# SSD scan of a two-block layer: earlier loads of decays and gates, stores moved to ScalarE's queue, input transposes in one-bank tiles

## Chip, cores, metric

The kernel runs on one core of one Trainium2 chip. The metric is device time in microseconds (us), the median of three runs; lower is better. The engines are named as in the profile: PE (TensorE matmul), PEld (its weight loads), DVE (VectorE), ACT (ScalarE), POOL (GpSimd), SP (SyncE, which here only issues transfers).

## What is computed

A sequence of 1024 tokens of width 1024 in fp32 passes through two blocks. The first block has a recurrent and attention layer and then an SSD (state space) layer; the second has a feed-forward part, a mixing layer and another feed-forward part. The change is in the SSD layer, whose scan works in 8 chunks of 128 tokens, for 4 groups of 8 heads:

```python
proj = x @ w_in                                   # z, xbc, dt
xs, bm, cm = split(silu(causal_conv(xbc)))        # inputs, B and C states
cs = cumsum(dt * a_neg) within a chunk
decay = exp(cs[l] - cs[s]) where s <= l
y_diag = ((C B^T) * decay) @ (xs * dt)            # inside a chunk
states = B^T @ (xs * dt * exp(cs[last] - cs))
y_off  = (C @ prev) * exp(cs); prev = prev * exp(cs[last]) + states
y = (y_diag + y_off + d_skip * xs) * silu(z)      # z: the gates
y = y * rsqrt(mean(y * y) per group) * norm_w
out = y @ w_out
```

## The kernel before

Every fp32 operand of a large product is split into a high and a low part, so a product is three matmuls (high with high, high with low, low with high). A scheduler puts the instructions of each engine into one fixed order when the kernel is built; `turn` and `issue_after` fix the order on PE. Each engine, and the queue of transfers on SP, works through its own list in order.

The SSD layer goes through 4 groups. A group has ten projection units, i = 0 to 9: two for B and C (`states`), four for the inputs (`inputs`), four for the gates (`gates`). A unit fills a two-bank PSUM tile `a` from a pool of two (`K.A`); ACT reads it out (L353 and L354 of the convolution, or L900 for a gate, which is then stored to DRAM at L901). `tokens` (L907) turns an input unit's result to tokens by rows: eight transposes (L914) into one more tile of `K.A`, two copies by ACT (L916).

While the units of group g run, the chunks of group g - 1 are worked off, one at the end of each unit (`chunk`, L992). Chunk n is made of:
- `within(n)`, called one chunk ahead: the decay row is loaded, spread over 128 partitions (L933, 512 KB), into a tile `s` of a pool of two; POOL subtracts (L934), DVE clips (L935), ACT takes the exponential (L936); PE makes C B^T and a transpose into a one-bank tile `pb` (L938, L939) of a pool of four (`K.B`); POOL scales the inputs (L942 to L944).
- `heads(n)`: 16 small matmuls (L952), added to y by DVE (L953).
- `between(n)`: the part from earlier chunks (L961, L962), the new state (L966, L968, L969), then the load of the chunk's gates (L972, 256 KB) into the buffer `xw`.
- `norm(n)`: y times gates on DVE (L976), square and sum on ACT (L978), the reciprocal root on DVE (L264 to L293), scaling on ACT (L980). `chunk(n)` calls `norm(n - 1)`.
- `flip(n)`: four transposes (L987) into `pb`, a copy on ACT (L988) and a store from SP (L989). It runs in the middle of the unit, two chunks later.

The last group's chunks have no units beside them. There, `early(i)` of `SsdOut` (L1062) is the company: 60 matmuls (L695) that multiply the rows of groups 0 to 2 that are ready with the output weights; their operands are streamed by `stream_rows` (load L708, split by ACT L140 and DVE L141), the sum is added by DVE (L1075) and stored (L1076). `prepare` (L1050) fills the weights: L1041 loads, L1043 (ACT) and L1044 (DVE) split. In the loop the order is `early(i)` with `flip(22 + i)` in its middle, then `chunk(24 + i)`. `rest` (L1078) then does the remaining rows and the layer norm.

Of the kernel before, what the change touches and what calls it, by code (L numbers as in the profile page):

```python
# [14 lines left out]
AF = mybir.ActivationFunctionType  # L15
ALU = mybir.AluOpType
AX = mybir.AxisListType

P = 128
# [148 lines left out]
def turn(K, trace):  # L168

    with K.tc.issue_after(anchor(K)):  # L170
        trace()
# [621 lines left out]
def ssd_layer(K, I, get, yd, out):  # L793

    nc = K.nc
# [28 lines left out]
    cs_d = K.DR([32, T])  # L824
# [24 lines left out]
    sz_d = [K.DR([T, 512]) for _ in range(4)]  # L849
    rf = [t.rearrange("p a b -> p (a b)") for t in (K.R2(), K.R2(), K.P2())]  # L850
    hv = lambda t: t.rearrange("p (h d) -> p h d", h=8)
    groups, held = {}, {}

    def column(c0, mid=None):
        a = K.A()
# [3 lines left out]
    def units(g):  # L859
        S = groups[g] = Ctx()  # L860
        S.fs = []

        def states(j, mid):
            c0, cj = ((4096 + g * P, 16 + g), (4608 + g * P, 20 + g))[j]
            if j == 0:
                S.bc = K.Q2()
            a = first if (g, j) == (0, 0) else column(c0, mid)
            conv4(K, S.bc[:, j, :], a, "s_conv_w", cj, 24, "s_conv_b", copy=True)
            nc.scalar.activation(S.bc[:, j, :], S.bc[:, j, :], AF.Silu)

        def inputs(m, mid):
            a = column(2048 + g * 512 + m * P, mid)
            f = K.L()
            conv4(K, f, a, "s_conv_w", 4 * g + m, 24, "s_conv_b", copy=True)
            nc.scalar.activation(f, f, AF.Silu)
            S.fs.append(f)

        def gates(hf, h, mid):
            if h == 0:
                c0 = g * 512 + hf * 256  # L880
                S.w = [wload(K, w_in[:, 4 * k:4 * k + 4, c0:c0 + 256], 4, 256) for k in range(2)]
            a = K.A()

            def quarters(qs):
                for q in qs:
                    o = a[:, q * 256:q * 256 + 256]
                    tk = slice((4 * h + q) * P, (4 * h + q + 1) * P)
                    for k in range(NK):
                        wh, wl = (S.w[k // 4][m][:, k % 4, :] for m in range(2))
                        xh, xl = get("h", k)[:, tk], get("l", k)[:, tk]  # L890
                        nc.tensor.matmul(o, xh, wh, start=k == 0, stop=False)  # L891
                        nc.tensor.matmul(o, xh, wl, start=False, stop=False)  # L892
                        nc.tensor.matmul(o, xl, wh, start=False, stop=k == NK - 1)  # L893

            quarters((0, 1))
            if mid is not None:
                turn(K, mid)
            turn(K, lambda: quarters((2, 3)))
            z = K.L()
            nc.scalar.activation(z, a, AF.Silu)  # L900
            nc.sync.dma_start(sz_d[g][4 * h * P:4 * h * P + 512, hf * 256:hf * 256 + 256].rearrange("(q p) c -> p q c", p=P),  # L901
                              z.rearrange("p (q c) -> p q c", q=4))

        return ([lambda mid, j=j: states(j, mid) for j in range(2)] + [lambda mid, m=m: inputs(m, mid) for m in range(4)]
                + [lambda mid, hf=hf, h=h: gates(hf, h, mid) for hf in range(2) for h in range(2)])

    def tokens(g, m):  # L907
        S = groups[g]
        if m == 0:
            mk = K.Q2 if g % 2 else K.P2  # L910
            S.xs = [mk().rearrange("p a (b c) -> p (a b) c", b=2) for _ in range(2)]
        b = K.A()
        for q in range(8):
            nc.tensor.transpose(b[:, q * P:(q + 1) * P], S.fs[m][:, q * P:(q + 1) * P], K.ident)  # L914
        for h in range(2):
            nc.scalar.activation(S.xs[h][:, :, m * P:(m + 1) * P],  # L916
                                 b[:, 512 * h:512 * h + 512].rearrange("p (q t) -> p q t", q=4), AF.Copy)

    def cols(g, c):
        k0 = (c % 2) * 128 + (c // 2) * 32 + 8 * g  # L920
        return lambda t, n: t[:, k0:k0 + 8].unsqueeze(2).to_broadcast([P, 8, n])

    def within(n):
        g, c = divmod(n, 8)
# [3 lines left out]
        X = groups[g].xs[c // 4][:, c % 4, :]  # L928
        r = rf[n % 3]
        xdt, xw, y, cbm, bt = r[:, 0:512], r[:, 512:1024], r[:, 1024:1536], r[:, 1536:1664], r[:, 1664:1792]  # L930
        m = K.S()
        mv = m.rearrange("p (h l) -> p h l", h=8)
        nc.sync.dma_start(mv, cs_d[8 * g:8 * g + 8, c * P:(c + 1) * P].partition_broadcast(P))  # L933
        nc.gpsimd.tensor_tensor(mv, mv, per_head(csT, P), ALU.subtract)  # L934
        nc.vector.tensor_scalar(m, m, 0.0, None, ALU.min)  # L935
        nc.scalar.activation(m, m, AF.Exp)  # L936
# [18 lines left out]
    def between(n):  # L955
# [8 lines left out]
        if c < 7:  # L964
# [4 lines left out]
                nc.vector.tensor_tensor(prev, prev, st, ALU.add)  # L969
            else:  # L970
                nc.vector.tensor_copy(prev, st)
        nc.sync.dma_start(xw, sz_d[g][c * P:(c + 1) * P, :])  # L972

    def norm(n):
        _, _, xdt, sz, y, _ = held[n]
        nc.vector.tensor_tensor(y, y, sz, ALU.mult)  # L976
        t = K.small(2, "yss", bufs=3)
        nc.scalar.activation(xdt, y, AF.Square, accum_out=t[:, 0:1])  # L978
        rsqrt_col(K, t[:, 1:2], t[:, 0:1], 1, 1.0 / 512, 1e-6)
        nc.scalar.activation(y, y, AF.Copy, scale=t[:, 1:2])  # L980

    def flip(n):
# [3 lines left out]
        for q in range(4):  # L986
            nc.tensor.transpose(yt[:, q * P:(q + 1) * P], y[:, q * P:(q + 1) * P], K.ident)  # L987
        nc.scalar.activation(xw, yt, AF.Copy)  # L988
        nc.sync.dma_start(yd[4 * g:4 * g + 4, :, c * P:(c + 1) * P].rearrange("m p t -> p m t"),  # L989
                          xw.rearrange("p (m t) -> p m t", m=4))  # L990

    def chunk(n):  # L992
        heads(n)
        between(n)
        if n % 8 < 7:
            within(n + 1)
        if n % 8:
            norm(n - 1)

    for g in range(4):
        for i, unit in enumerate(units(g)):
            n = 8 * g - 8 + i
            mid = (lambda n=n: flip(n - 2)) if g and i > 1 else None
            with K.tc.issue_after(anchor(K)) if g + i else nullcontext():
                unit(mid)
            if g == 0 and i == 4:
                turn(K, steps)
            if g and i < 8:  # L1010
                turn(K, lambda: chunk(n))
            if 3 <= i < 7:
                turn(K, lambda: tokens(g, i - 3))
            if g and i == 8:
                norm(n - 1)
            if i == 8:
                turn(K, lambda: within(8 * g))
    out.prepare()
    for i in range(NT):
        turn(K, lambda: out.early(i, (lambda: flip(22 + i)) if i > 1 else None))  # L1020
        turn(K, lambda: chunk(24 + i))
    norm(31)
    return flip


class SsdOut:
# [20 lines left out]
    def half(self, i):  # L1047
        return self.yh[:, 512 * (i % 2):512 * (i % 2) + 512]

    def prepare(self):  # L1050
        K = self.K
        self.an = [anchor(K)] * 2
        xw = [K.X() for _ in range(4)]
        for k in (8, 9):
            self.fill(k)
        for k in range(8):
            self.fill(k, xw[k // 4][:, k % 4, :], xw[2 + k // 4][:, k % 4, :])
        for k in (10, 11):
# [19 lines left out]
    def rest(self, flip):  # L1078
# [14 lines left out]
        for i in range(NT):  # L1093
# [4 lines left out]
            with deferred(K, an[i]):  # L1098
                yv = dict(zip((10, 11), stream_rows(K, self.yd, 10, i, self.half(i), n=2)))
                yv.update(zip(range(12, 16), stream_rows(K, self.yd, 12, i)))  # L1100
                nc.sync.dma_start(z, self.zd[i * P:(i + 1) * P, :])
            out_tile(K, a, [w[k] for k in order], lambda k: yv[order[k]], 6, 3, (lambda: flip(30 + i)) if i < 2 else None)
            an.append(anchor(K))
            nc.vector.tensor_tensor(z, z, a, ALU.add)
            layernorm(K, z, g, b, i < 6)
# [856 lines left out]
```

## Time and profile before

| | us |
|---|---|
| median of 3 runs | 3326.03 (3321.61 to 3326.29) |
| the profiled execution, device time | 3326.46 |
| its span in the trace | 3324.6 |
| PE busy | 3087.2 (93% of the span) |
| DVE busy | 2226.4 (67%) |
| ACT busy | 1626.6 (49%) |
| POOL busy | 780.1 (23%) |
| projection units of the SSD layer | 540 to 1126 |
| its last group's chunks, beside `early` | 1126 to 1312 |

Times in the rows count from the start of the span. A busy PE is not a PE at its peak, since matmuls overlap. A wait is idle time of an engine, put down to the work that released it. The granted clock is TensorE's, 1.00 being 2.4 GHz; its other level is 1.2 GHz.

### The profile page before, as it was taken

The page shows a single profiled execution, that of the slowest core. Times are in us where ns is not written, and L with a number is a line of the kernel's source. Part 1 is how long each engine was busy: PE and PEld are TensorE (multiplying, and loading weights), DVE is VectorE, ACT ScalarE, POOL GpSimd, SP SyncE. Part 2 cuts the span into 40 slices and gives each one's busy share as a digit, 9 for nine tenths or more (in the row PEclk, how much of TensorE's full clock was granted, in tenths as well). Part 3 has the DMA queues.
Part 4 walks back from the last instruction along what each step waited for, and adds up shares of the span by engine and source line. Part 5 has one row for each costly group of instructions (what it writes and reads, how often), then busy time and mean ns, then how long its engine had stood idle before and what let it go on. Part 6 is the DMA issues. An engine that isn't in the chain of part 4 may idle for free. (4 is left out here: it accounts for less than half of the span.)

```text
span 3324.6 us, 42105 instructions
## 1 busy us (share of the span) xinstructions
PE 3087.2 (93%) x15560; PEld 2575.9 (77%) x15560; DVE 2226.4 (67%) x3605; ACT 1626.6 (49%) x2947; POOL 780.1 (23%) x487
## 2 busy tenths in 40 slices
PE   8999899999999888789999999899898799999998
PEld 6878777878887766677778777688787588888776
DVE  6537777375848445887775689735676955555997
ACT  5526634354645422555555444642465755554442
POOL 0000011122323121532223435100000433232543
PEclk9999999999999899989999999999999899999999
DMA  3157343234435545323332620445553422224322
GB/s 128 57 194 231 104 145 89 75 86 110 102 102 100 162 136 160 101 74 127 120 122 83 234 81 3 159 141 201 144 158 118 171 76 83 89 76 139 121 83 114
DMA packets 344957, 398.96 MB, mean 120 GB/s; under 512 B 20656, under 2 KB 270640, under 8 KB 344752
## 3 DMA queue, kind: packets, MB, share of 16 engines
q1 hardware_dynamic: 344752, 396.28, 38.3%
q8 instruction: 123, 2.02, 0.2%
q14 instruction: 82, 0.67, 0.1%
HBM read 279.29 MB, written 116.92 MB: 119 GB/s over the span
## 5 line engine op out<-in xcount | busy, mean ns | idle before, releaser
L141 DVE TENSOR_TENSOR wlo<-wst,whi 128x1024 fp32r<-128x1024 f32 (+1 forms) x190 | 232.3, 1226 | 349.5 <-ACT whi L140 339.0
L185 PE MATMUL pa<-x,whi 128*128 128x512 f32 x1568 | 429.4, 395 | 14.6 <-ACT l L354 10.2
L185 PEld LDWEIGHTS pa<-x,whi 128*128 128x128 f32 x1568 | 292.1, 189 | 78.4 <-ACT l L354 11.4
L140 ACT ACTIVATE whi<-wst 128x1024 fp32r<-128x1024 f32 (+1 forms) x190 | 180.0, 949 | 345.8 <-PE pa L185 85.6
L147 ACT ACTIVATE wst<-wst,pk 128x128 f32<-128x128 f32 (+1 forms) x816 | 251.7, 392 | 187.8 <-DMA wst<-in_ffn_w_in_dram 115.5
L185 PE MATMUL pa<-x,wlo 128*128 128x512 f32 x784 | 244.1, 392 | 0.8 <-DVE wlo L141 0.7
L1268 PE MATMUL pb<-x,whi 128*128 128x512 f32 (+1 forms) x736 | 224.3, 381 | 0.3 <-DVE r L141 0.3
L1268 PE MATMUL pa<-x,whi 128*128 128x512 f32 (+1 forms) x736 | 220.2, 382 | 0.6 <-ACT p L1271 0.2
L1347 PE MATMUL pa<-wlo,whi 128*128 128x512 f32 x768 | 188.4, 403 | 15.6 <-DVE wlo L141 12.8
L1347 PE MATMUL pb<-wlo,whi 128*128 128x512 f32 x744 | 182.5, 403 | 13.4 <-DVE wlo L141 13.4
L1231 POOL TENSOR_TENSOR s<-wst 128x512 f32<-128x512 f32 x44 | 57.7, 1311 | 564.5 <-ACT wst L147 526.8
L1347 PEld LDWEIGHTS pa<-wlo,whi 128*128 128x128 f32 x768 | 148.7, 195 | 52.5 <-DVE wlo L141 17.7
L1347 PEld LDWEIGHTS pb<-wlo,whi 128*128 128x128 f32 x744 | 144.0, 195 | 48.0 <-DVE wlo L141 17.7
L934 POOL TENSOR_TENSOR s<-s,p 128x1024 f32<-128x1024 f32 x32 | 61.9, 1936 | 488.5 <-DMA s<-d 401.8
L185 PEld LDWEIGHTS pa<-x,wlo 128*128 128x128 f32 x784 | 147.4, 188 | 34.3 <-DVE wlo L141 2.4
L891 PE MATMUL pa<-whi,x 128*128 128x256 f32 x512 | 149.5, 292 | 9.0 <-ACT l L900 7.6
L1268 PEld LDWEIGHTS pa<-x,whi 128*128 128x128 f32 x736 | 135.4, 188 | 28.3 <-ACT p L1271 1.1
L1268 PEld LDWEIGHTS pb<-x,whi 128*128 128x128 f32 x736 | 136.2, 188 | 27.0 <-DVE r L141 0.5
L140 ACT ACTIVATE whi<-s 128x1024 fp32r<-128x1024 f32 x88 | 93.0, 1057 | 115.1 <-POOL s L1232 67.0
L893 PE MATMUL pa<-whi,x 128*128 128x256 f32 x512 | 146.2, 286 | 0.0
L892 PE MATMUL pa<-wlo,x 128*128 128x256 f32 x512 | 146.1, 285 | 0.0
L1268 PE MATMUL pa<-x,wlo 128*128 128x512 f32 (+1 forms) x368 | 140.0, 381 | 1.5 <-DVE wlo L141 1.5
(577 smaller groups left out, 7966.4 us busy)
## 6 DMA issues: line engine op xcount, KB each, us to landing
wst<-in_ffn_w_in_dram SPq DMA_DIRECT2D x88, 512.0 KB, 3.8
d<-l SPq DMA_DIRECT2D x83, 512.0 KB, 3.3
d<-p SPq DMA_DIRECT2D x82, 512.0 KB, 3.5
x<-d SPq DMA_DIRECT2D x128, 256.0 KB, 5.4
p<-d SPq DMA_DIRECT2D x46, 512.0 KB, 4.6
wst<-in_s_w_in_dram SPq DMA_DIRECT2D x40, 512.0 KB, 4.1
s<-d SPq DMA_DIRECT2D x32, 512.0 KB, 9.5
l<-d SPq DMA_DIRECT2D x24, 512.0 KB, 5.6
```

Source lines behind the costliest of these rows:

```text
L140: K.nc.scalar.activation(hi, src, AF.Copy)
L141: (eng or K.nc.vector).tensor_tensor(lo, src, hi.bitcast(F32), ALU.subtract)
L147: K.nc.scalar.activation(st[:, k, :], st[:, k, :], AF.Copy, scale=col(K, gain, k0 + k))
L185: K.nc.tensor.matmul(ps[:, h:h + 512], w, x[:, h:h + 512], start=k == 0 and m == 0, stop=k == n - 1 and m == 2)
L891: nc.tensor.matmul(o, xh, wh, start=k == 0, stop=False)
L892: nc.tensor.matmul(o, xh, wl, start=False, stop=False)
L893: nc.tensor.matmul(o, xl, wh, start=False, stop=k == NK - 1)
L934: nc.gpsimd.tensor_tensor(mv, mv, per_head(csT, P), ALU.subtract)
L1231: G(s1, a21, a22, ALU.add)
L1268: nc.tensor.matmul(p, l[:, k, :], r[:, k, :], start=k + m == 0, stop=k == 3 and m == 2)
L1347: nc.tensor.matmul(bank[j], th[:, a + o:a + o + P], tw[:, b:b + 512], start=c + m == 0, stop=c == n - 1 and m == 2)
```

## The change

- The decay rows are loaded by a function of their own (`decays`), called two chunks ahead: for chunks 0 and 1 before the units, for n + 2 in `chunk(n)` right after `heads(n)`.
- The gates of a chunk are loaded by `gate`, in two transfers of 128 KB into spare columns of the three working buffers: for chunk n + 1 inside `norm(n)`, right after the multiplication by the gates of n, which is now two half-width multiplications.
- `chunk(n)` calls `norm(n)` and no longer `norm(n - 1)`.
- The stores of the gates (L901) and of the outputs (L989) are issued from ACT's queue.
- `tokens` uses two one-bank tiles of `K.B`, four transposes and one copy each, and no tile of `K.A`; it runs in the middle of the next unit, behind `flip`, and no longer after the chunk.
- The weights 8 and 9 of `SsdOut` are loaded and split in unit 8 of the last group (`ahead`).
- In the last group, `chunk(24 + i)` goes ahead of `early(i)`, which has `flip(23 + i)` in its middle; `rest` has one flip left.

```diff
--- before.py
+++ after.py
@@ -849,7 +849,7 @@
     sz_d = [K.DR([T, 512]) for _ in range(4)]
     rf = [t.rearrange("p a b -> p (a b)") for t in (K.R2(), K.R2(), K.P2())]
     hv = lambda t: t.rearrange("p (h d) -> p h d", h=8)
-    groups, held = {}, {}
+    groups, held, rows = {}, {}, {}
 
     def column(c0, mid=None):
         a = K.A()
@@ -898,7 +898,7 @@
             turn(K, lambda: quarters((2, 3)))
             z = K.L()
             nc.scalar.activation(z, a, AF.Silu)
-            nc.sync.dma_start(sz_d[g][4 * h * P:4 * h * P + 512, hf * 256:hf * 256 + 256].rearrange("(q p) c -> p q c", p=P),
+            nc.scalar.dma_start(sz_d[g][4 * h * P:4 * h * P + 512, hf * 256:hf * 256 + 256].rearrange("(q p) c -> p q c", p=P),
                               z.rearrange("p (q c) -> p q c", q=4))
 
         return ([lambda mid, j=j: states(j, mid) for j in range(2)] + [lambda mid, m=m: inputs(m, mid) for m in range(4)]
@@ -909,16 +909,20 @@
         if m == 0:
             mk = K.Q2 if g % 2 else K.P2
             S.xs = [mk().rearrange("p a (b c) -> p (a b) c", b=2) for _ in range(2)]
-        b = K.A()
-        for q in range(8):
-            nc.tensor.transpose(b[:, q * P:(q + 1) * P], S.fs[m][:, q * P:(q + 1) * P], K.ident)
         for h in range(2):
-            nc.scalar.activation(S.xs[h][:, :, m * P:(m + 1) * P],
-                                 b[:, 512 * h:512 * h + 512].rearrange("p (q t) -> p q t", q=4), AF.Copy)
+            b = K.B()
+            for q in range(4):
+                nc.tensor.transpose(b[:, q * P:(q + 1) * P], S.fs[m][:, (4 * h + q) * P:(4 * h + q + 1) * P], K.ident)
+            nc.scalar.activation(S.xs[h][:, :, m * P:(m + 1) * P], b.rearrange("p (q t) -> p q t", q=4), AF.Copy)
 
     def cols(g, c):
         k0 = (c % 2) * 128 + (c // 2) * 32 + 8 * g
         return lambda t, n: t[:, k0:k0 + 8].unsqueeze(2).to_broadcast([P, 8, n])
+
+    def decays(n):
+        g, c = divmod(n, 8)
+        mv = rows[n] = K.S().rearrange("p (h l) -> p h l", h=8)
+        nc.sync.dma_start(mv, cs_d[8 * g:8 * g + 8, c * P:(c + 1) * P].partition_broadcast(P))
 
     def within(n):
         g, c = divmod(n, 8)
@@ -928,9 +932,8 @@
         X = groups[g].xs[c // 4][:, c % 4, :]
         r = rf[n % 3]
         xdt, xw, y, cbm, bt = r[:, 0:512], r[:, 512:1024], r[:, 1024:1536], r[:, 1536:1664], r[:, 1664:1792]
-        m = K.S()
-        mv = m.rearrange("p (h l) -> p h l", h=8)
-        nc.sync.dma_start(mv, cs_d[8 * g:8 * g + 8, c * P:(c + 1) * P].partition_broadcast(P))
+        mv = rows.pop(n)
+        m = mv.rearrange("p h l -> p (h l)")
         nc.gpsimd.tensor_tensor(mv, mv, per_head(csT, P), ALU.subtract)
         nc.vector.tensor_scalar(m, m, 0.0, None, ALU.min)
         nc.scalar.activation(m, m, AF.Exp)
@@ -969,11 +972,20 @@
                 nc.vector.tensor_tensor(prev, prev, st, ALU.add)
             else:
                 nc.vector.tensor_copy(prev, st)
-        nc.sync.dma_start(xw, sz_d[g][c * P:(c + 1) * P, :])
+
+    def gate(n):
+
+        held["z"] = [rf[(2 * n + h) % 3][:, 1792:2048] for h in range(2)]
+        for h, z in enumerate(held["z"]):
+            nc.sync.dma_start(z, sz_d[n // 8][n % 8 * P:(n % 8 + 1) * P, 256 * h:256 * h + 256])
 
     def norm(n):
-        _, _, xdt, sz, y, _ = held[n]
-        nc.vector.tensor_tensor(y, y, sz, ALU.mult)
+        _, _, xdt, _, y, _ = held[n]
+        for h, z in enumerate(held["z"]):
+            yh = y[:, 256 * h:256 * h + 256]
+            nc.vector.tensor_tensor(yh, yh, z, ALU.mult)
+        if n % 8 < 7:
+            gate(n + 1)
         t = K.small(2, "yss", bufs=3)
         nc.scalar.activation(xdt, y, AF.Square, accum_out=t[:, 0:1])
         rsqrt_col(K, t[:, 1:2], t[:, 0:1], 1, 1.0 / 512, 1e-6)
@@ -986,41 +998,46 @@
         for q in range(4):
             nc.tensor.transpose(yt[:, q * P:(q + 1) * P], y[:, q * P:(q + 1) * P], K.ident)
         nc.scalar.activation(xw, yt, AF.Copy)
-        nc.sync.dma_start(yd[4 * g:4 * g + 4, :, c * P:(c + 1) * P].rearrange("m p t -> p m t"),
+        nc.scalar.dma_start(yd[4 * g:4 * g + 4, :, c * P:(c + 1) * P].rearrange("m p t -> p m t"),
                           xw.rearrange("p (m t) -> p m t", m=4))
 
     def chunk(n):
         heads(n)
+        if n < 30:
+            decays(n + 2)
         between(n)
         if n % 8 < 7:
             within(n + 1)
-        if n % 8:
-            norm(n - 1)
-
+        norm(n)
+
+    decays(0)
+    decays(1)
 
 
     for g in range(4):
+        def middle(i):
+            if g and i > 1:
+                flip(8 * g - 10 + i)
+            if 4 <= i < 8:
+                tokens(g, i - 4)
+
         for i, unit in enumerate(units(g)):
-            n = 8 * g - 8 + i
-            mid = (lambda n=n: flip(n - 2)) if g and i > 1 else None
             with K.tc.issue_after(anchor(K)) if g + i else nullcontext():
-                unit(mid)
+                unit((lambda: middle(i)) if i > 1 + 2 * (not g) and (g or i < 8) else None)
             if g == 0 and i == 4:
                 turn(K, steps)
             if g and i < 8:
-                turn(K, lambda: chunk(n))
-            if 3 <= i < 7:
-                turn(K, lambda: tokens(g, i - 3))
-            if g and i == 8:
-                norm(n - 1)
+                turn(K, lambda: chunk(8 * g - 8 + i))
             if i == 8:
+                if g == 3:
+                    out.ahead()
                 turn(K, lambda: within(8 * g))
+        gate(8 * g)
     out.prepare()
     for i in range(NT):
-        turn(K, lambda: out.early(i, (lambda: flip(22 + i)) if i > 1 else None))
         turn(K, lambda: chunk(24 + i))
-    norm(31)
-    return flip
+        turn(K, lambda: out.early(i, (lambda: flip(23 + i)) if i else None))
+    return lambda: flip(31)
 
 
 class SsdOut:
@@ -1047,12 +1064,14 @@
     def half(self, i):
         return self.yh[:, 512 * (i % 2):512 * (i % 2) + 512]
 
+    def ahead(self):
+        for k in (8, 9):
+            self.fill(k)
+
     def prepare(self):
         K = self.K
         self.an = [anchor(K)] * 2
         xw = [K.X() for _ in range(4)]
-        for k in (8, 9):
-            self.fill(k)
         for k in range(8):
             self.fill(k, xw[k // 4][:, k % 4, :], xw[2 + k // 4][:, k % 4, :])
         for k in (10, 11):
@@ -1099,7 +1118,7 @@
                 yv = dict(zip((10, 11), stream_rows(K, self.yd, 10, i, self.half(i), n=2)))
                 yv.update(zip(range(12, 16), stream_rows(K, self.yd, 12, i)))
                 nc.sync.dma_start(z, self.zd[i * P:(i + 1) * P, :])
-            out_tile(K, a, [w[k] for k in order], lambda k: yv[order[k]], 6, 3, (lambda: flip(30 + i)) if i < 2 else None)
+            out_tile(K, a, [w[k] for k in order], lambda k: yv[order[k]], 6, 3, flip if i == 0 else None)
             an.append(anchor(K))
             nc.vector.tensor_tensor(z, z, a, ALU.add)
             layernorm(K, z, g, b, i < 6)
```

## Rows read from the trace of the kernel before

**Rows 1.** The page: busy time of each engine, its share, its instructions.
```profile
PE 3087.2 (93%) x15560; PEld 2575.9 (77%) x15560; DVE 2226.4 (67%) x3605; ACT 1626.6 (49%) x2947; POOL 780.1 (23%) x487
```
**Rows 2.** Busy time by stretch; columns: PE, PEld, DVE, ACT, POOL, clock, DMA, GB/s.
```profile
540.00:1126.00 586.00, 562.78 (x3435) 491.72 (x3434) 359.78 (x521) 296.51 (x366) 148.21 (x106) 0.99 0.39 95
1158.00:1312.00 154.00, 136.08 (x622) 108.26 (x622) 80.48 (x142) 38.17 (x68) 27.27 (x21) 0.94 0.46 136
...
1175.10:1193.10 18.00, 18.00 (x89) 14.54 (x89) 10.17 (x20) 4.78 (x9) 1.04 (x1) 1.00 0.63 169
1193.10:1309.80 116.70, 98.78 (x437) 77.57 (x436) 59.19 (x104) 27.75 (x51) 24.32 (x19) 0.93 0.39 118
```
**Rows 3.** Waits of PE, 1158 to 1312: total us, times, longest.
```profile
PE pb L938 <- ACT r L988: 13.0, 4, 3.5
PE pb L938 <- ACT p L988: 3.4, 1, 3.4
```
**Rows 4.** Timeline of SP's queue: start, duration, line, transfer.
```profile
1207.40 0.39 SPq L933 DMA_DIRECT2D s<-d  x1
1207.88 1.00 SPq L972 DMA_DIRECT2D p<-d  x1
...
1222.93 0.37 SPq L989 DMA_DIRECT2D d<-r  x1
1223.39 0.46 SPq L708 DMA_DIRECT2D q<-d  x1
...
1229.49 0.33 SPq L1076 DMA_DIRECT2D d<-l  x1
1229.91 0.39 SPq L933 DMA_DIRECT2D s<-d  x1
```
**Rows 5.** Timeline of POOL, same period; in brackets, idle time and its releaser.
```profile
1216.67 1.90 POOL L934 TENSOR_TENSOR s<-s,p 128x1024 f32<-128x1024 f32 x1 [12.75 <-DMA s<-d]
```
**Rows 6.** Timeline of DVE, same period.
```profile
1217.29 1.82 DVE L976 TENSOR_TENSOR p<-p 128x512 f32<-128x512 f32 x1 [5.41 <-DMA p<-d]
...
1228.25 1.21 DVE L1075 SCALAR_TENSOR_TENSOR l<-l,pa 128x1024 f32<-128x1024 f32 x1
```
**Rows 7.** Timeline of ACT, same period.
```profile
1219.14 0.63 ACT L978 ACTIVATE p<-p 128x512 f32<-128x512 f32 x1 [9.28 <-DVE p L976]
...
1222.33 0.58 ACT L988 ACTIVATE r<-pb 128x512 f32<-128x512 f32 x1
1226.43 0.63 ACT L140 ACTIVATE q<-q 128x512 fp32r<-128x512 f32 x1 [3.53 <-DMA q<-d]
```
**Rows 8.** Timeline of PE in the two periods.
```profile
1186.18 7.07 PE L695 MATMUL pa<-x,q 128*128 128x512 f32 x30
...
1222.96 0.49 PE L938 MATMUL pb<-q 128*128 128x128 f32 x2 [2.98 <-ACT r L988]
```
**Rows 9.** Waits of PE, 540 to 1126.
```profile
PE pa L185 <- ACT l L354: 10.2, 5, 3.9
PE pa L891 <- ACT l L900: 7.6, 4, 3.7
PE pa L185 <- ACT l L900: 2.2, 1, 2.2
PE pa L891 <- ACT l L354: 1.3, 1, 1.3
```
**Rows 10.** Line L901: duration min/median/max in ns, first and last start.
```profile
L901 SPq DMA_DIRECT2D d<-l x16: 359/360/370, 621.6 to 1132.9; - x16
```
**Rows 11.** Timeline of PE and DVE in a unit of the third group.
```profile
1077.24 1.90 PE L952 MATMUL pb<-r,s 128*128 128x64 f32 x16
...
1087.67 0.68 DVE L969 TENSOR_TENSOR p<-p,pb 128x512 f32<-128x512 f32 x1
```
**Rows 12.** Weight fills of `prepare`, by line, as Rows 10.
```profile
L1043 ACT ACTIVATE x<-wst,pk x8: 1147/1150/1158, 1126.6 to 1153.3; 128x1024 fp32r<-128x1024 f32 x8
```
**Rows 13.** Waits of PE, 1312 to 1340.
```profile
PE pb L987 <- ACT r L980: 1.6, 1, 1.6
```

## The prediction

> **What bounds the kernel now.** I began with the busy times: PE has work 93% of the span, DVE 67%, ACT 49% [rows 1]. So a gain has to come from time in which PE waits or runs at the low clock, and the question is where that lies. The table by stretch shows two different stages [rows 2]. Beside the units (540 to 1126) PE is busy 562.8 of 586 us at a granted clock of 0.99. In the last group (1158 to 1312) it is busy 136.1 of 154 at 0.94. Inside the last group the periods differ: one of 18.0 us has PE busy throughout at clock 1.00, and the five after it take 116.7 us together, 23.3 each. The work is the same, so 18.0 us is what PE needs, shown by the trace itself.
>
> The waits of PE name the cause: 16.4 us in five waits, all of L938 on ACT's L988 [rows 3]. L938 is the first matmul of `within`. A period takes five one-bank tiles (flip, L952, L961, L966, L938) from a pool of four, so L938 gets the bank of the flip, and L988 is the copy that empties it. Why is L988 late? The timelines of one period answer, and should be read as a ring. SP issues the decay load L933 at 1207.40 and the gate load L972 right behind it [rows 4]. POOL starts L934 at 1216.67, released by that load, 9.3 us after its issue [rows 5]. DVE's L976 waits for the gates until 1217.29 [rows 6], ACT's L978 for L976 until 1219.14, and L988, two steps behind L978 in ACT's order, starts at 1222.33 [rows 7]. At 1222.96 PE goes on [rows 8]. The ring closes on SP: the store L989 (1222.93) has to be issued before the stream load L708 (1223.39) [rows 4], that load releases ACT's L140 at 1226.43 [rows 7], then comes DVE's L1075 at 1228.25 [rows 6], then the store L1076 at 1229.49, and behind it the next L933 at 1229.91 [rows 4]. From L933 to L933 is 22.5 us. The last group runs at the pace of this ring, two load latencies and a line of engines, and PE waits inside it.
>
> In the unit stage PE waits 21.3 us in eleven waits for L354 or L900 [rows 9]. Both are ACT's reading of a two-bank tile `a`. With the tokens' tile between two units, a pool of two hands each unit the tile of the unit directly before it, which ACT has only the time of one chunk to empty.
>
> **The change part by part.** The base is the profiled execution, 3326.46 us (span 3324.6 and 1.86 around it), 0.43 above the median of the three runs.
>
> *Loads ahead (tail).* With the decays two chunks ahead, L933 is issued a period and more before POOL needs it: 9.3 us of latency against 18. With the gates a period ahead, L976 meets landed data. Both cuts of the ring are needed and both are made; L988 then follows its transposes. Five periods fall from 116.7 to 90 at best: 26.7 us. Below it is nothing, if another ring closes. What is late next: the stream load for the next `early`. If L708 stands behind L1076, the path from the end of `early` is L1075 1.2, L1076 0.3, L708 0.5 and 3.0 to landing (1223.39 to 1226.43), L140 0.6, and as much again for DVE's part, about 6.3 us by these rows; PE has until then the chunk and 12 matmuls. Thirty matmuls take 7.07 us [rows 8], so 60 take 14.1, the chunk 18.0 - 14.1 = 3.9 and 12 matmuls 2.8: 6.7. It just fits, so I take off 0.5 us in each of the five, an estimate: **24** (0 to 26.7).
>
> *Chunk before `early`; `ahead`.* After the last unit the weights of rows 0 to 7 are filled, eight splits from 1126.6 to 1153.3, 3.8 us apart [rows 12]. `early(0)` cannot end before the last, so filling 8 and 9 sooner does not shorten this stretch. But chunk 24 (3.9 us, a little less for a first chunk) now runs inside it instead of after it, while its DVE work may hold up the splits. **3** (0 to 4).
>
> *Small banks and earlier reading (units).* The unit tiles now alternate alone, so a unit meets the tile of the unit before last, whose matmuls ended a unit and a chunk ago (48 x 0.236 + 3.9, some 15 us); and ACT is no longer held before L978 by gates in flight. The 21.3 us of waits go, and with them most of the low clock: 0.99 over 586 us is 1% of it, 5.9. Upper bound 27.2. Against it: a token period takes seven one-bank tiles from the pool of four, so the tokens' second tile gets the bank that DVE's L969 reads. In a late unit L969 ends 11.1 us after the start of L952 (1077.24 to 1088.35) [rows 11]. PE would want that bank after 3.9 of chunk, half a unit of 24 matmuls (5.7), the flip and four transposes (some 0.9): 10.5. That is 0.6 us of wait in a late unit; in all 12 token periods beside chunks it makes 7.2. **20** (0 to 27).
>
> *Stores on ACT.* 16 gate stores and 32 output stores, 0.36 us each where SP issues them now [rows 10]: 48 x 0.36 = 17.3 us of ACT. No row shows ACT issuing a transfer; the nearest is SP's own. I charge nothing, because ACT is busy 296.5 of 586 us and 38.2 of 154 [rows 2] and its data are its own, ready when the store comes up; with that cover gone it costs 17.3. Queued behind such a store on ACT is the next copy or split, 0.36 us later.
>
> The Trainium skill, DMA: Bandwidth & Descriptors, section Issuing engines are not separate DMA queues, speaks against this part: transfers started by different engines run on the same DMA engines, so a second issuer saves only the time of issuing. By that rule the move buys nothing here and the sum would lose ACT's 17.3. The trace agrees that issuing is short (0.36 us); that loads stood behind L989 while it waited for ACT is a wait in SP's order, which the rule does not price.
>
> *New waits on SP.* The load of the decays n + 2 waits for `heads(n)` on PE, and the second gate load for the multiplication of n on DVE. Behind them stand weight loads, L708, L1076. Before, the same places waited for L988 and L1075. I charge nothing; the rivals price it.
>
> *Halved multiplications.* 32 more on DVE. Each half can cost no more than the whole, 1.82 in the slow form [rows 6]: at most 58 us, at least nothing, against 300 us of idle DVE [rows 2]. Nothing. The 32 additional gate loads go to SP, 0.36 each by the same row as the stores, 11.5 us in 770: nothing.
>
> *One flip fewer in `rest`.* Its wait for L980, 1.6 us [rows 13], goes. **1.6** (0 to 1.6).
>
> Sum: 24 + 3 + 20 + 1.6 = 48.6; 3326.46 - 48.6 = 3277.9, so **3278**.
>
> **The rivals.**
> 1. *The units gain nothing* (17%). The eleven waits move from `pa` to `pb` tiles, since DVE is no less loaded there (359.8 of 586) and `norm(n)` now stands in the period of its own chunk, where ACT's L978 waits for DVE. For: L969 at 11.1 us. Against: an idle DVE before L976 is what made it late. 3326.5 - 24 - 3 - 1.6 = 3298.
> 2. *Another ring in the tail* (14%). L1075 or the gate load's wait on DVE comes 4 us later than I count, PE waits for the stream split in each of five periods: 20 us of the 24 are given back. For: the slack above is 0.4 us. Against: without L989 on SP, L708 can be issued as soon as PE has read the old rows, during `early`. 3278 + 20 = 3298.
> 3. *ACT pays for its stores* (6%): the 17.3 fall on PE's path. 3295. For: no row shows ACT issuing. Against: ACT idles half of the unit stage and three quarters of the tail.
> 4. *It does not do what it says* (4%): both 1 and 2, with 24 + 20 gone: 3278 + 40 = 3318 and beyond, up to no change.
> 5. *Slower* (7%): the bank ring of seven on four. It decides if DVE reads the state bank (L969) late in each of the 12 token periods: with the 20 gone, the other 28.6 are used up at 2.4 us of wait per period, and it is 6.7 slower at 2.9, which is L969 ending 13.4 us after L952 where the row has 11.1. At 3.1 the time is 3335. For: `norm(n)` adds DVE work right there. Against: the bank's readers stand ahead of `norm` in the chunk.
>
> **How the numbers follow.** The forecast has 52%. Its own range: with all bounds reached, 26.7 + 4 + 27.2 + 1.6 = 59.5, 3267; five less, because chunk 31's work on DVE (10.2 us in a period [rows 2], take half) now lies before the last `early` and no longer before the layer norm of `rest`: 3262. Upwards, with 18 in the tail and 10 in the units, 3294. The 80% range reaches over rivals 1 to 3 and leaves out 4 and 5: 3262 to 3304. A difference under 0.2% (6.7 us) can hardly be told from none here. Faster: cases 0 to 3, 89%. Same: 4%. Slower: 7%.
>
> **What would show it.** Right: periods of the last group of 18 to 18.6 us; POOL's L934 and DVE's L976 no longer released by loads; no wait of L938 on L988; the clock near 1.00 between 1150 and 1300. In the units, no wait of L185 or L891 on L354 or L900. Chunk 24 ahead of `early(0)`, whose end still follows the eighth split. Wrong: waits of PE on `pb` tiles, released by L962, L969 or the tokens' copies (rival 1 or 5); the last group at 20 us and more with L695 waiting for L140 or L141 (rival 2); L988 or L354 late behind a store on ACT (rival 3).

## The result, and the profile after

The changed kernel takes 3287.95 us (median of four runs, 3284.85 to 3290.19) against 3325.45 (four runs, 3321.61 to 3326.29): a ratio of 0.9891, 95% interval 0.9876 to 0.9905. It is 37.5 us faster; 3278 had been forecast, and 10 us of the forecast gain are missing. The profiled execution took 3289.96 us with a span of 3288.2. In it the lines of `decays` and `within` are L925 and L937 to L948, of `heads` L955 and L956, the gate load is L980, `norm` L986 to L992, `flip` L999 to L1001, the fills L1058 to L1061, the sum of `early` and its store L1094 and L1095; L140, L141, L185, L695, L708 and L891 to L901 keep their numbers.

The busy times of the page answer to [rows 1]:

```profile
PE 3082.6 (94%) x15560; PEld 2572.9 (78%) x15560; DVE 2210.6 (67%) x3637; ACT 1625.5 (49%) x2945; POOL 779.2 (24%) x487
```

PE has as many matmuls as before and is 4.6 us less busy in a span that is 36.4 us shorter; what went is mostly waiting and low clock. DVE, with 32 more instructions, is 15.8 us less busy. The stages, each from the start of one matmul to that of another (first and last matmul of the units, first matmul of `rest`, last of the output rows in `rest`), in the profiled executions:

| us | before | after | gain | forecast |
|---|---|---|---|---|
| units | 581.6 | 565.5 | 16.0 | 20 |
| last group, with `early(7)` and chunk 31, to the start of `rest` | 186.0 | 170.1 | 15.8 | 27 |
| `rest` | 84.0 | 79.1 | 4.9 | 1.6 |

Together about 36.8 us; the spans differ by 36.4. Ahead of the units the trace after is 5.3 us longer and behind `rest` 4.9 shorter; that code is the same in both. These are single executions, and the units vary: in four of the experiments below (e1, e3, e7, e8) the engines go through the units in the same order as in the changed kernel, but for one weight load and its split in e1, and the units take 568.3, 572.5, 572.0 and 571.9 us. So 565.5 is a short one, and a difference under some 7 us in the units shows nothing.

Busy time by stretch, as [rows 2]: the units, the last group, and two of its periods.

```profile
544.00:1115.00 571.00, 559.58 (x3439) 488.39 (x3438) 342.29 (x545) 296.86 (x367) 145.56 (x106) 1.00 0.38 99
1115.00:1285.00 170.00, 152.58 (x689) 119.49 (x689) 96.72 (x174) 53.02 (x86) 30.28 (x22) 0.94 0.57 174
1149.00:1167.00 18.00, 18.00 (x89) 14.56 (x88) 11.51 (x17) 5.35 (x9) 2.92 (x2) 1.00 0.61 212
1185.00:1208.00 23.00, 19.85 (x89) 15.69 (x88) 11.01 (x22) 4.72 (x9) 7.64 (x6) 0.93 0.50 152
```

In the units PE now idles 11.4 of 571 us and the granted clock is 1.00. In the last group the period of 18.0 us with PE busy throughout is there again, but also one of 23.0. The starts of the chunks' first matmul give all periods: before 17.0, 17.9, 23.2, 22.8, 23.2, 24.0, 23.4 (26.6 us above 18.0 in five of them); after, from chunk 25 on, 18.0, 18.0, 22.9, 18.7, 22.7, 19.2 (11.5 above in four).

The waits of PE, first 520 to 1115 (the largest, L212 at 4.1 us, left out: it belongs to the layer ahead), then 1115 to 1290:

```profile
PE pb L841 <- DVE p L840: 4.0, 1, 4.0
PE pa L185 <- DVE wlo L141: 2.0, 4, 0.7
PE pa L892 <- DVE wlo L141: 1.9, 2, 1.2
...
PE pb L941 <- ACT r L1000: 7.1, 3, 3.1
PE pa L695 <- ACT l L140: 4.7, 1, 4.7
PE pa L695 <- DVE x L1061: 3.1, 3, 2.2
```

In the units the 21.3 us of [rows 9] are gone, and nothing waits for a bank that L972 (before L969) reads. In the last group the wait of [rows 3] is still there under its new numbers, L941 on L1000: 7.1 us, and 0.5 in a fourth wait, where it was 16.4.

Why it is still there is read from the timeline of one period, all engines, as [rows 4 to 8]:

```profile
1167.10 1.89 PE L955 MATMUL pb<-p,s 128*128 128x64 f32 x16
...
1173.44 1.21 DVE L1094 SCALAR_TENSOR_TENSOR l<-l,pa 128x1024 f32<-128x1024 f32 x1
1174.68 0.33 SPq L1095 DMA_DIRECT2D d<-l  x1
...
1175.11 0.38 SPq L925 DMA_DIRECT2D s<-d  x1
...
1185.47 1.90 POOL L937 TENSOR_TENSOR s<-s,p 128x1024 f32<-128x1024 f32 x1 [12.50 <-DMA s<-d]
1187.40 1.52 DVE L938 TENSOR_SCALAR s<-s 128x1024 f32<-128x1024 f32 x1 [6.08 <-POOL s L937]
1188.95 1.06 ACT L939 ACTIVATE s<-s 128x1024 f32<-128x1024 f32 x1 [6.87 <-DVE s L938]
...
1191.25 0.58 ACT L1000 ACTIVATE r<-pb 128x512 f32<-128x512 f32 x1
...
1191.88 0.50 PE L941 MATMUL pb<-q 128*128 128x128 f32 x2 [3.15 <-ACT r L1000]
1192.33 0.63 ACT L140 ACTIVATE q<-q 128x512 fp32r<-128x512 f32 x1 [0.50 <-ACT r L1000]
...
1193.93 1.21 DVE L1094 SCALAR_TENSOR_TENSOR l<-l,pa 128x1024 f32<-128x1024 f32 x1
1195.17 0.33 SPq L1095 DMA_DIRECT2D d<-l  x1
1195.62 0.37 SPq L925 DMA_DIRECT2D s<-d  x1
```

It is a ring again, and a shorter one: from L925 to L925 20.5 us, before 22.5. It has one load latency where there were two: the decay load (L925) lands after 10 us, POOL, DVE and ACT follow, L1000 stands behind L939 in ACT's order, L140 behind L1000, DVE's sum L1094 behind the split in DVE's order, its store L1095, and behind the store on SP the next L925. The gates are no longer in it. And the decays, called a chunk earlier, are issued no earlier: POOL still waits for them. The group of POOL's subtraction, before and after (count, busy and mean, idle time ahead of it and its releasers):

```profile
L934 POOL TENSOR_TENSOR s<-s,p 128x1024 f32<-128x1024 f32 x32 | 61.9, 1936 | 488.5 <-DMA s<-d 401.8 <-DVE p L839 62.8 <-ACT q L869 12.6
```
```profile
L937 POOL TENSOR_TENSOR s<-s,p 128x1024 f32<-128x1024 f32 x32 | 64.5, 2016 | 448.1 <-DMA s<-d 337.5 <-DVE p L839 64.3 <-DVE r L986 23.7
```

So the time did not come from where the forecast took it, and the experiments ask which part brought it.

### The profile page after: what moved, and what is told of

Same layout as the page of the kernel before. It is cut to its first block, busy times and chain, and to the rows that moved or that the text cites. A ratio compares the mean times of both kernels' runs of the same rounds, so it can differ in the third digit from the quotient of the medians.

```text
span 3288.2 us, 42188 instructions
## 1 busy us (share of the span) xinstructions
PE 3082.6 (94%) x15560; PEld 2572.9 (78%) x15560; DVE 2210.6 (67%) x3637; ACT 1625.5 (49%) x2945; POOL 779.2 (24%) x487
## 5 line engine op out<-in xcount | busy, mean ns | idle before, releaser
L141 DVE TENSOR_TENSOR wlo<-wst,whi 128x1024 fp32r<-128x1024 f32 (+1 forms) x190 | 234.1, 1235 | 355.2 <-ACT whi L140 337.2
L185 PE MATMUL pa<-x,whi 128*128 128x512 f32 x1568 | 428.6, 394 | 1.8 <-DVE l L141 0.9
L140 ACT ACTIVATE whi<-wst 128x1024 fp32r<-128x1024 f32 (+1 forms) x190 | 179.9, 948 | 350.9 <-PE pa L185 85.7
L185 PEld LDWEIGHTS pa<-x,whi 128*128 128x128 f32 x1568 | 291.5, 188 | 63.9 <-DVE x L141 1.7
L185 PE MATMUL pa<-x,wlo 128*128 128x512 f32 x784 | 244.0, 392 | 2.0 <-DVE wlo L141 2.0
L185 PEld LDWEIGHTS pa<-x,wlo 128*128 128x128 f32 x784 | 147.2, 188 | 36.1 <-DVE wlo L141 4.5
L937 POOL TENSOR_TENSOR s<-s,p 128x1024 f32<-128x1024 f32 x32 | 64.5, 2016 | 448.1 <-DMA s<-d 337.5
L140 ACT ACTIVATE whi<-s 128x1024 fp32r<-128x1024 f32 x88 | 93.0, 1057 | 112.6 <-POOL s L1251 59.9
L891 PE MATMUL pa<-whi,x 128*128 128x256 f32 x512 | 147.9, 289 | 0.0
L681 POOL TENSOR_TENSOR p<-p,q 128x1024 f32<-128x1024 f32 x8 | 21.1, 2643 | 513.7 <-DVE p L680 476.8
```

The lines of the kernel that those rows point to most:

```text
L140: K.nc.scalar.activation(hi, src, AF.Copy)
L141: (eng or K.nc.vector).tensor_tensor(lo, src, hi.bitcast(F32), ALU.subtract)
L185: K.nc.tensor.matmul(ps[:, h:h + 512], w, x[:, h:h + 512], start=k == 0 and m == 0, stop=k == n - 1 and m == 2)
```

## The experiments

"After" is the changed kernel; ratios are to the kernel before, timed on the same chip. Stage times are of the profiled executions, with the bounds of the table above.

**1. Undo the calls ahead: the decays (e1), the gates (e7).**

```diff
 e1     def within(n):
+        decays(n)
         mv = rows.pop(n)
 ...
-        if n < 30:
-            decays(n + 2)
```


> The changed kernel with the load of the decay rows called again inside within, one chunk ahead, as before. Theory of the ring: the pool of two decay tiles sets when the load can start (after heads two chunks earlier), wherever it is called; the last group stays at periods of 18 to 23 us and the time at 3288, give or take 4. Rival, the step of the prediction: the call two chunks ahead is what shortened the ring; then the periods go back to about 22 us and the time to 3300 or more.

```diff
 e7     def norm(n):
-        if n % 8 < 7:
-            gate(n + 1)
 ...     within(n + 1)
+        gate(n)
         norm(n)
```


> The changed kernel with the gates of a chunk loaded in its own chunk, right before their multiplication. Theory of the ring: the multiplication waits for a load again, in DVE's order ahead of the clip of the decays and in ACT's order ahead of the flip's copy; the last group back at 22 to 23 us a period and some waits in the units; 3298 to 3310. Rival: the decay load sets the pace in any case and the gates hide beside it; 3288 to 3292.

Measured: 0.9883 (0.9867 to 0.9900) and 0.9876 (0.9861 to 0.9890), neither to be told from 0.9891; units 568.3 and 572.0, last group 169.5 and 170.3. Neither call ahead is worth anything by itself, because neither changes when the load goes out. SP's timeline of e1 (the sum's store is its L1092) shows it for the decays:

```profile
1173.72 0.33 SPq L1092 DMA_DIRECT2D d<-l  x1
1174.16 0.38 SPq L925 DMA_DIRECT2D s<-d  x1
```

Called one chunk ahead, the load stands at the same place, right behind the sum's store. Its tile comes from a pool of two and is free when `heads` has read it (1169.0 after, by the first line of the ring), whichever chunk calls it; the scheduler had already issued it as early as that allows, and what holds it is SP's order.

In e7 the gate loads go out where they did, right behind the multiplication of the chunk before and a period ahead of their own (timelines of e7, DVE and SP; the first of the two transfers):

```profile
1185.34 0.42 DVE L986 TENSOR_TENSOR p<-p 128x256 f32<-128x256 f32 x1
1185.45 0.33 SPq L980 DMA_DIRECT2D r<-d  x1
...
1204.97 0.42 DVE L986 TENSOR_TENSOR r<-r 128x256 f32<-128x256 f32 x1
```

DVE's multiplication waits for no load in e7, as in the changed kernel. So e7 did not take back what it was meant to: the gates are early because they have a buffer of their own, and e7 keeps that. What early gates are worth is not shown by it.

**2. Where the last group's ring closes: the sum's store on ACT's queue (e3), the decay load on POOL's (e2).**

```diff
 e3
-        nc.sync.dma_start(self.zd[i * P:(i + 1) * P, :], x)
+        nc.scalar.dma_start(self.zd[i * P:(i + 1) * P, :], x)
 e2 (in decays)
-        nc.sync.dma_start(mv, cs_d[...].partition_broadcast(P))
+        nc.gpsimd.dma_start(mv, cs_d[...].partition_broadcast(P))
```


> The changed kernel with the store of early's sum issued from ACT. Theory of the ring: SP no longer waits for DVE's sum ahead of the decay load; the load starts up to 6 us sooner, periods near 18 us, time 3276 to 3284. Rival: ACT now waits in its order for DVE's sum ahead of the next split, and the ring only moves from SP to ACT: 3288 or slower.

> The changed kernel with the decay rows loaded from POOL's queue. Theory of the ring: on SP this load stands behind the store of early's sum, some 6 us after its tile is free; on POOL it starts when the tile is free, the exponential and the flip's copy behind it come sooner, the waits of the bank in the last group (7.6 us and three low-clock stretches) go, periods near 18 us, time 3276 to 3282. Rival: the load's own latency of 10 us sets the pace, or POOL pays for issuing; then no gain or a loss of up to 10 us.

e3 gives 0.9852 (0.9832 to 0.9872), 3284.82 us; its interval lies below that of the changed kernel. The load now goes out ahead of the store, and five periods together have PE busy all of 89.8 us at full clock (timeline and busy time by stretch of e3):

```profile
1177.70 0.45 SPq L925 DMA_DIRECT2D s<-d  x1
1182.34 0.34 ACTq L1095 DMA_DIRECT2D d<-l  x1
```
```profile
1155.50:1245.30 89.80, 89.80 (x437) 72.67 (x436) 59.36 (x109) 28.73 (x50) 24.39 (x18) 1.00 0.65 183
```

All periods from chunk 25 on are 17.9 to 18.0, the last group 158.1. This shows the ring: with that one link out, all of the 11.5 us is gone.

e2 gives 0.9994 (0.9982 to 1.0006). The last group gains a little (167.0), but the units lose 42.6 us (608.1), which neither forecast had: both looked at the last group. The waits of PE and of POOL in e2, 520 to 1130:

```profile
PE pb L915 <- ACT r L944: 20.0, 4, 6.3
PE pb L915 <- ACT p L944: 8.6, 2, 4.9
```
```profile
POOL s L925 <- PE pb L955: 90.8, 15, 31.7
```

The load waits for PE's `heads`, now in the order of an engine with work of its own, and POOL stands still 90.8 us in 15 waits. That this is what makes ACT's L944 late was not tried apart.

**3. The stores alone: both back on SP (e4), only the gates' back (e12), both moved in the kernel before (e9).**

```diff
 e4: both; e12: the first only; e9: the reverse of both, in the kernel before
-            nc.scalar.dma_start(sz_d[g][...], z...)
+            nc.sync.dma_start(sz_d[g][...], z...)
-        nc.scalar.dma_start(yd[4 * g:4 * g + 4, ...], xw...)
+        nc.sync.dma_start(yd[4 * g:4 * g + 4, ...], xw...)
```


> The changed kernel with gates and outputs stored from SP again. Theory of the ring: the stream load of early waits behind the output store for ACT's copy again, its 3.5 us of latency come back into the ring, periods of the last group near 22 us; time 3296 to 3304. Rival: a second issuer saves only issuing time; 3288, give or take 4, or a little less because ACT is spared 17 us of issuing.

> The changed kernel with the gate stores (L901) alone back on SP; the output stores stay on ACT's queue. With both back, the units lost 27.7 us and the last group 10.8. The first theory is that it is L901 that held the decay load of the units (it was issued at 935.18, 0.46 us ahead of the load, in that run) and L989 that held the loads of the last group, where no gate is stored: the units lose 20 to 28 us and the last group nothing, ratio 0.995 to 0.998. The rival: the output stores held SP in the units too, so that L901 alone costs little there: ratio 0.989 to 0.993.

> The kernel before with one part of the change alone: the gate stores (L901) and the output stores (L989) are issued from ACT's queue. The first theory (loads stood behind stores in SP's order, and the moved stores carry the gain, but the tokens in a two-bank tile keep the waits for L354 and L900) expects the last group to gain about as in the changed kernel, 10 to 15 us, and the units little, 0 to 8: ratio 0.993 to 0.997. If the moved stores suffice without the small banks, both stages gain, about 33 us: 0.989 to 0.991. If they need the other parts of the change (loads called ahead, order) nothing comes: 0.998 to 1.002.

e4: 0.9990 (0.9981 to 0.9999). All the rest of the change, without this part, is worth 0.1%. The units take 593.2, the last group 180.9, `rest` 84.1. The theory's 3296 to 3304 is a ratio of 0.991 to 0.994; it fell short because it had the last group alone in view. One place in the units, first e4, then the changed kernel (timelines, SP, POOL, DVE, ACT, PE):

```profile
935.18 0.37 SPq L901 DMA_DIRECT2D d<-l  x1
935.64 0.46 SPq L925 DMA_DIRECT2D s<-d  x1
...
947.08 1.90 POOL L937 TENSOR_TENSOR s<-s,p 128x1024 f32<-128x1024 f32 x1 [17.05 <-DMA s<-d]
...
949.73 1.06 ACT L939 ACTIVATE s<-s 128x1024 f32<-128x1024 f32 x1 [9.25 <-DVE s L938]
950.70 0.58 ACT L1000 ACTIVATE r<-pb 128x512 f32<-128x512 f32 x1
...
951.33 2.07 PE L964 MATMUL pb<-p,q 128*128 128x512 f32 x2 [5.67 <-ACT r L1000]
```
```profile
921.27 0.53 SPq L925 DMA_DIRECT2D s<-d  x1
...
927.14 0.37 ACTq L901 DMA_DIRECT2D d<-l  x1
...
930.98 2.29 POOL L937 TENSOR_TENSOR s<-s,p 128x1024 f32<-128x1024 f32 x1 [9.08 <-DMA s<-d]
```

In e4 the decay load stands behind the gate store, which waits for ACT's L900; the subtraction, the exponential and, behind it in ACT's order, the flip's copy L1000 come late, and PE waits for the flip's bank. In the changed kernel the load goes out 5.9 us ahead of that store. That SP was held like this in the kernel before is in its waits there, 520 to 1130:

```profile
SPq L989 <- ACT r L988: 119.8, 16, 16.0
SPq L989 <- ACT p L988: 61.1, 8, 15.3
SPq L901 <- ACT l L900: 52.6, 11, 12.4
SPq L901 <- ACT r L941: 38.2, 3, 14.1
```

These four rows make 271.7 us in which every load behind had to wait too.

e12: 0.9942 (0.9924 to 0.9960), between the two forecasts, so that the ratio does not decide. The stages do: the last group is untouched, 169.8 against 170.1, and the units take 590.4, close to e4's 593.2; with the outputs' stores back too (e4), the last group is 11.1 us longer and `rest` 5.4. So the gates' stores hold the units and the outputs' stores the last group, as the first theory said. The units' loss of 24.9 us is from an execution that is the slowest of the six, 10 above their median; the median is only 0.5% above the changed kernel's.

e9: 0.9954 (0.9936 to 0.9972), as the first theory said. The last group takes 171.7, 14.3 of the changed kernel's gain of 15.8 there; the units 579.4, 2 us of its 16. The waits of [rows 9] stay, 18.0 us in nine (waits of PE in e9, 520 to 1115):

```profile
PE pa L185 <- ACT l L354: 9.2, 4, 3.2
PE pa L891 <- ACT l L900: 7.5, 4, 3.8
PE pa L891 <- ACT l L354: 1.3, 1, 1.3
```

**4. The small banks: tokens in a two-bank tile again (e5), small banks alone (e6), small banks and stores (e10).**

```diff
 e5 (e6 the reverse, in the kernel before; e10 = e6 and e9)
-            b = K.B()            # twice, 4 transposes and one copy each, mid-unit
+        b = K.A()                # once, 8 transposes, two copies, behind the chunk
```


> The changed kernel with the tokens' transposes in a two-bank tile after the chunk again, as before. Theory: the pool of two makes each unit wait for ACT's reading of the unit directly before it, as before: waits of L185 and L891 on ACT of about 20 us and some low clock; 3300 to 3308. Rival: those waits came from ACT being held by gates in flight, which the early gate loads removed; 3288 to 3294.

> The kernel before with only the tokens' transposes moved into one-bank tiles in the middle of the next unit. Theory: the units' share of the gain comes from this alone, 14 to 18 us; the last group as before; 3308 to 3312. Rival: without early gates the banks fill with ACT's late copies and half or more is lost; 3316 to 3326.

> The kernel before with two parts of the change: both stores on ACT's queue, and the tokens in one-bank tiles in the middle of the next unit. Decays, gates, weights 8 and 9 and the order of the last group stay as before. The first theory (these two parts, each needing the other, are the whole change) expects the changed kernel's time: ratio 0.987 to 0.991. If the loads called ahead or the order carry a part that the single returns did not show, because each can stand in for the other, it is 0.992 to 0.997.

e5: 0.9936 (0.9919 to 0.9952). The units go up to 590.9, the last group stays (167.8); PE's waits for L354 and L900 are back, 29.1 us. So in the changed kernel the small banks do what was forecast of them. e6: 1.0018 (1.0008 to 1.0028): alone they cost, 597.1 in the units. The waits of PE in e6, 540 to 1130, show the price (L960 is the changed kernel's L964, L987 its L1000):

```profile
PE pb L960 <- ACT r L987: 13.8, 2, 7.4
PE pb L960 <- ACT p L987: 6.5, 1, 6.5
```

It is the bank of the flip, late as in e4 and e12; both kinds of store are on SP here, and that it is the gate stores again was not tried apart. With seven tiles on four banks PE comes back to this bank soon. e10: 0.9942 (0.9920 to 0.9964), units 572.7, last group 170.4, `rest` 87.7. With the stores moved these waits fall to 3.7 us and the small banks gain. But by the ratio this is half of the change's gain, not all of it. Of the span 12.1 us are missing: 8.6 in `rest`, 0.3 in the last group and 7.2 in the units, less 4 outside these stages; the 7.2 show nothing, since e3 and e8, with the changed kernel's units, take as long as e10 there. The first theory, that these two parts are the whole, falls by its ratio.

**5. The order of before (e8), and the sum's store without the loads ahead (e11).**

```diff
 e8
+        turn(K, lambda: out.early(i, (lambda: flip(22 + i)) if i > 1 else None))
         turn(K, lambda: chunk(24 + i))
-        turn(K, lambda: out.early(i, (lambda: flip(23 + i)) if i else None))
 ... (`rest` has two flips again)
 e11 = e10, and the sum's store from ACT's queue as in e3
```


> The changed kernel with early ahead of chunk in the last group's loop, as before, flips two chunks behind. Theory: the order is worth chunk 24 hidden in the weight fills (2 to 3 us) and the shorter start of rest (3 to 5 us): 3293 to 3297. Rival: the order is what shortened the ring; then 3300 and more.

> As the run with both stores and the small banks, and the store of the sums of early (L1076) too is issued from ACT's queue. If the ring of the last group is closed by the decay load behind that store, and by nothing that the earlier loads or the new order cut, its periods come down to about 18.0 us as in the run that moved this store in the changed kernel: ratio 0.983 to 0.988. If the gate load, which in this kernel still goes out within its own chunk, closes a ring of its own (L976 released by it late), the periods stay at 20 us or more: 0.988 to 0.993.

e8: 0.9893 (0.9878 to 0.9908), the changed kernel's ratio; the last group takes 169.7 and `rest` 83.2. So the new order gains 4.1 us in `rest`, as its theory said of the start of `rest`, and nothing in the last group; in the ratio it does not show. e11: 0.9901 (0.9874 to 0.9927), the spread of its runs too wide to set it apart from the changed kernel; the ratio lies where the second forecast had it, but by the periods it is the first that holds. Its last group is the shortest of all, 155.5 (units 576.2, `rest` 83.2), every period from chunk 26 on at 17.9 to 18.0 (busy time by stretch of e11, five periods):

```profile
1171.00:1261.00 90.00, 90.00 (x437) 72.78 (x436) 59.44 (x111) 27.94 (x51) 25.15 (x19) 1.00 0.57 169
```

Here the decays and the gates are called and buffered as in the kernel before. So the last group reaches what PE needs with three stores off SP's queue and no load called earlier.

## Why the prediction was right, and where it was wrong

The direction and the range were right, and so were the ring as a way of reading the last group and 18.0 us as its floor (e3, e11). That the total came within 10 us is in part luck: the largest term rested on a step that failed, and the part that carries the gain was put at nothing. By its steps:

- *Loads ahead (tail), 24.* The step that failed: "With the decays two chunks ahead, L933 is issued a period and more before POOL needs it", and with it "Both cuts of the ring are needed and both are made". The decay load is issued when its tile is free and SP has come past the store ahead of it; calling it earlier changes neither (e1). The gates' cut was made: DVE waited 78.7 us in 23 waits for gates before and not at all after. But it is not needed: e9, with DVE waiting for gates, has the last group at 171.7, e11 at 155.5. What cut the ring was a part costed at nothing, L989 off SP's queue. It cuts one link, not all, and the ring closes over L1076. This is rival 2, another ring, at about half its price: 15.8 of the 27 us came. Its wording was off too: it is not the gate load or the stream load that closes it, but the decay load behind the sum's store.
- *Chunk before `early`; `ahead`, 3.* From the last matmul of the units to the last of `early(0)` it took 31.7 before and takes 33.6 with chunk 24 in it; with 3.9 for the chunk, 2.0 gained. The size agrees, but not for the reason given: e6, e8 and e9, all with the order of before, get there in 27.7, 27.9 and 26.4, so that with chunk 24 behind it they are sooner than 33.6. The new order gains nothing here; what shortened this stretch in those three was not tried.
- *Small banks (units), 20.* The waits went as said (21.3 to 0), the clock rose from 0.99 to 1.00, 16.0 came in the profiled execution (9 to 13 in the four others with the same units); e5 shows that this part is needed. What was missed is that it holds only with the gate stores off SP (e4, e6, e12). Rival 5 was right that seven tiles on four banks can make the change slower, and e6 is slower; but the late reader is ACT's L1000, not DVE's L969, and in the changed kernel no such wait is left.
- *Stores on ACT, 0.* Their cost was rightly put at nothing (0.366 us an issue on ACT, and no wait of PE put down to it). Their gain was not: undone they take back nearly all (0.9891 to 0.9990, 33 us), alone they bring 0.46%, 15 us. The prediction saw that "loads stood behind L989 while it waited for ACT is a wait in SP's order", and gave it no term. The Trainium skill, DMA: Bandwidth & Descriptors, section Issuing engines are not separate DMA queues, puts the worth of a second issuer at the time of issuing. By that, 48 issues of 0.36 us would be 17.3, and taking the stores back costs about twice as much: the time comes from SP's list, which goes in order, so that a store that waits for its data holds the loads behind it. Here the measurement decides.
- *New waits on SP, 0.* Nearly right: SP waits 247.6 us for L980 in the units (113.2, 54.1 and 80.3, waits of SP, 520 to 1130), and the waits of PE that are left there are small. The largest that may follow from it are those for weight splits (L141), 3.9 us where it was 0.7; the cause was not tried.
- *Halved multiplications, 0.* Never run alone, but the traces show that they shortened DVE's work (groups of DVE, 540 to 1126 before and 544 to 1115 after):

```profile
L976 DVE TENSOR_TENSOR r<-r 128x512 f32<-128x512 f32 x16 | 24.6, 1539 | 32.5 <-DMA r<-d 32.5
```
```profile
L986 DVE TENSOR_TENSOR r<-r,r 128x256 f32<-128x256 f32 x16 | 6.7, 418 | 0.0
```

  All whole ones of the units took 37.3 us, all halves take 20.0, and DVE is busy 342.3 us there, 359.8 before. The fastest whole one took 0.68 us, so what went is the slow form; why, no run shows.
- *One flip fewer in `rest`, 1.6.* 4.9 came. The wait of [rows 13] is gone, as said; e8 takes back 4.1. That the greater part is work of chunk 31 on DVE, which now lies ahead of `rest` (DVE 62.6 us busy in `rest` before, 59.4 after), fits and was not tried. The prediction had this as 5 us in its lower bound and not in its sum.

A slip in its sums: rival 4 takes off 40 where its own words, 24 and 20, make 44; that would be 3322.

What stays open: stores and small banks give half, each of the calls ahead and the order taken back alone gives nothing, and yet together the rest is worth 0.5% (0.9942 to 0.9891; with the sum's store moved in both, 0.9901 to 0.9852). Four things were in all of e1, e7 and e8 and in none of e9 to e11: the gates in a buffer of their own, which brings them early (in e10 DVE still waits 64.3 us for gates), the halved multiplications, `norm(n)` in the period of its own chunk, and the weights 8 and 9 in unit 8. None was run alone, and that some of them and the order stand in for each other is not excluded.

## What to carry to other kernels

When PE waits inside a ring, list every instruction on the ring's in-order queues, and ask of each transfer what stands ahead of it there; a store that waits for its data holds back each load behind it, and moving that store to the queue of the engine that makes the data was worth more here than calling the load earlier. A load called earlier is issued earlier only if its buffer is free by then: with a pool of two, look at when the tile was last read, before counting a gain. After undoing a part, look in the trace whether it is undone: e1 and e7 took back a call, and the loads went out where they had. Undo parts in pairs too: small banks alone were slower by 0.2%, stores alone faster by 0.5%, and neither alone tells what the change does.

## What was unexpected

- A transfer issued from ACT's queue takes 0.366 us there, as from SP's (0.360); from POOL's queue the same decay load takes 0.925 us to issue (median of 32), where SP takes 0.447, and lands no sooner (9.7 against 9.5 us).
- The decay load, one row spread over 128 partitions (512 KB), lands after 9.5 us in the median where the two largest groups of weight loads of 512 KB take 3.8 and 4.1 (transfers of the page after).
